# Weight splits without GpSimd, a gate applied to the product, and feed-forward rows scaled beforehand

## The chip, the cores and the metric

One core of one Trainium2 chip runs the kernel. The engines are named as the profile names them: PE is TensorE (PEld its weight loads), DVE VectorE, ACT ScalarE, POOL GpSimd, SP SyncE, which issues most DMAs. The metric is the device time of one execution in microseconds (us); the stated time is the median of three.

## The reference

Three transformer-like blocks follow one another on 256 rows of 1024 numbers, all in fp32. Cut to what matters here:

```python
def first_block(x, ...):                       # one layer
    proj = rms_norm(x, norm_w) @ w_in          # attention of two kinds, gates
    merged = sigmoid(gm) * (y_a @ w_branch_a) + sigmoid(gn) * (y_b @ w_branch_b)
    return x + merged @ w_out

def second_block(x, c, ctx, ...):              # two layers, m = six modulation vectors a layer
    h = h + m[2] * mixer(modulate(rms_norm(h), m[0], m[1]))   # layer 0: attention and convolution; layer 1: short convolution
    h = h + m[5] * ec_moe(modulate(rms_norm(h), m[3], m[4]))  # 16 experts, 32 rows each

def third_block(x, mem, ...):                  # two layers
    x = x + concat(mix, cross) @ w_out         # difference attention; gated linear attention
    x = x + conv_ffn(rms_norm(x, ffn_norm))

def conv_ffn(h, w_up, conv_w, conv_b, w_down):
    u = h @ w_up                               # 1024 -> 5632
    a, g = split(causal_conv_of_3_rows(u, conv_w) + conv_b)
    return (silu(g) * a) @ w_down              # 2816 -> 1024
```

The gate of the second block's mixers is m[2], a vector of 1024 by which the columns of a product are multiplied.

## The kernel before

**Dense products.** A dense weight is cut into groups of columns, and a group into slabs of up to 2048 floats a partition, each loaded by one DMA of SP into a ring of 4 (in the second block 7) places. `weights` (L384) cuts a slab into pieces of 1024 floats a partition and splits each: ACT casts it to the high half wh (fp32r, L378), and the low half wl = w - wh (L379) is made by DVE or by POOL. A counter decides (L404): of three splits POOL makes two, and in the difference attention, the third block's first mixer, all (`SHARES = 3, 2` and `DIFF_SHARES = 1, 1`). wh and wl have three buffers each. PE then does three products for each tile of 128 rows of the weight: high with high (L413), high with low (L414), low with high (L415). In `columns`, used by the feed-forward, the short convolution and others, the weight is the stationary operand and the 256 rows of data run through; in `rows` the data are stationary.

**The gate.** `residual` adds a product to x. Where a gate mrow is given (the mixers of the second block, ev_out and sc_out), `weights` multiplies each loaded slab in place by the gate's columns before it splits it: POOL the even slabs, DVE the odd ones (L395). The splits of such slabs are DVE's alone.

**The feed-forward** (`conv_ffn`, one for each layer of the third block). The rows x, times the norm's gain, are there turned and split (xh, xl), but not divided by their root mean square: this factor, rr, takes a chain of small operations on DVE (L532, L343 to L353), a product (ndiag) and a copy, and is applied to the product. The first products, called up, are done in 22 groups of 256 columns: 48 products for a group, into two PSUM banks (tag acc, of which there are three). For each bank DVE multiplies by rr into SBUF (ffu, L1941), ACT applies the third tap and the bias (ffc, L1943), and DVE adds the two other taps (L1944, L1945); then the two halves meet (ffh, L1949 to L1951) and are split into ff_h and ff_l (L381, L382). The second products, down, follow.

**Order.** The program is written engine by engine from a simulated schedule when it is built, so an engine's order isn't that of the code; each engine runs its own list strictly in order, and waits on semaphores.

Of the kernel before, what the change touches and what calls it, by code (L numbers as in the profile page):

```python
# [31 lines left out]
# Dense weights: (input name, layer, row order or None, column groups, k tiles a slab)  # L32
# [70 lines left out]
class Cols:  # L103
    """Columns of a [128, n] array: name -> slice."""
# [18 lines left out]
def _t5(n):  # L123
    # n < 16 exact, then the places where the logarithmic bucket steps up
    return n if n < 16 else min(15 + sum(n >= b for b in T5_STEPS), 31)
# [12 lines left out]
def _col(v):  # L138
    """A vector as [128, n]: element i*128+p at [p, i]."""
    return np.asarray(v).reshape(-1, 128).T  # L140


def _tables(i):
    """For each block, constants that depend on shapes alone and the small vectors and
    matrices, laid out for the partitions they are used on."""
# [90 lines left out]
# of so many splits of weights, how many GpSimd does  # L236
SHARES = 3, 2
# layer 0's slabs of modulation weights up to which the first block takes; those on VectorE; how many at a time
# [3 lines left out]
DIFF_SHARES = 1, 1  # L242


class Parts:
    """[128, 8, n] in tiles of its own for each few columns, so that they can take turns
    with those of another one of the same tag."""
# [13 lines left out]
class Later:  # L261
    """Parts from column k0 on."""
# [8 lines left out]
class Kern:  # L271
    def __init__(self, tc, ctx, a, tabs):
# [8 lines left out]
        self.fill, self.due, self.pace, self.nsplit, self.nslab, self.loads = None, 0, PACE[0], 0, 0, []  # L281
        self.tab, self.shares, self.hb = {}, SHARES, 1
# [39 lines left out]
    def slab(self, n):  # L322
        """The next place of n floats a partition in the ring of weights."""
        at = self.turn % sum(c for _, c in self.rings)
        self.turn += 1
        for pool, c in self.rings:
            if at < c:
                return pool.tile([128, 2048], F32, tag="w", name="w")[:, :n]
            at -= c

    def step(self, n=1):
        """Gives way to work that runs beside the products."""
# [6 lines left out]
    def newton(self, x, n, pool=None):  # L339
        """1 / sqrt(x)"""  # L340
# [15 lines left out]
    def rsqrt(self, ss, n, dim, pool=None):  # L356
        """1 / sqrt(ss / dim + EPS)"""
# [4 lines left out]
    def across(self, col, pool, name):  # L362
        """[128, n] -> PSUM [128, 128 * n]: element i * 128 + p along the rows of every partition."""
# [11 lines left out]
    def split(self, hi, lo, src, scale=1.0, eng=None):  # L375
        """hi + lo = scale * src, with hi and lo as the single-pass products take them."""
        if isinstance(scale, float) and scale == 1.0:
            self.nc.scalar.copy(hi, src)  # L378
            (eng or self.nc.vector).tensor_tensor(lo, src, hi.bitcast(F32), op=OP.subtract)  # L379
# [5 lines left out]
    def weights(self, key, g, chunks=None, by=None, gain=None):  # L385
        """Slabs of a column group, times a row [128, width] or a column [128, k tiles]:
        (k0, nk, width, high part, low part)."""
        for at, k0, nk, width in (OFF[key][g] if chunks is None else [OFF[key][g][c] for c in chunks]):
# [5 lines left out]
            if by is not None:  # L394
                (self.nc.vector if self.nslab % 2 else self.nc.gpsimd).tensor_tensor(w, w, by[:, None, :].to_broadcast([128, nk, width]), op=OP.mult)  # L395
            step = min(nk, 1024 // width)
            for k in range(0, nk, step):
# [3 lines left out]
                self.nsplit += 1  # L401
# [3 lines left out]
                else:  # L405
                    self.split(wh, wl, w[:, k:k + m], eng=self.nc.gpsimd if by is None and self.nsplit % self.shares[0] < self.shares[1] else None)
# [10 lines left out]
    def rows(self, key, g, xs, nkt, evac, ps=None, chunks=None, by=None, gain=None):  # L417
        """Rows of tokens: two tiles of 128 rows."""
# [4 lines left out]
        for k0, nk, width, wh, wl in self.weights(key, g, chunks, by, gain):  # L423
# [9 lines left out]
    def columns(self, key, g, xs, nkt, evac, m=128, n=S):  # L433
        """Columns of tokens: tiles of m outputs by 256 tokens (and what else the columns hold)."""
        width = OFF[key][g][0][3]
        ps = [self.acc(f"{key}{i}") for i in range(width // m)]
# [10 lines left out]
    def residual(self, key, xs, nkt, mrow=None, pool=None, hook=None, gain=None):  # L447
        """x += xs @ w (times mrow), and what the next norm needs of x."""
# [3 lines left out]
        def evac(g):  # L452
            def f(i, p):
                c = slice(512 * g, 512 * g + 512)
                nc.vector.tensor_tensor(self.x[:, i, c], self.x[:, i, c], p, op=OP.add)  # L455
# [7 lines left out]
        if nch == 2:  # L463
            ps = self.four(key)
            ps = [ps[:2], ps[2:]]
            for c in range(2):
                for g in range(2):
                    by = None if mrow is None else mrow[:, 512 * g:512 * g + 512]
                    self.rows(key, g, xs, nkt, evac(g) if c else None, ps[g], [c], by)
# [12 lines left out]
    def norm_state(self, pool=None, tag="xl", gain=None, fp=None, n=2, shift=None):  # L482
        """Sums of squares by tile and part (n of them), and the raw rows turned (in turns with the low part);
        with a gain [128, 8], their products with it instead, split at once, and a shift behind them, twice."""
# [8 lines left out]
    def norm_part(self, ns, x, g, w):  # L493
        """Columns w * g and on of x: [128, 2, D], or two tiles"""
# [43 lines left out]
    def norm_columns(self, ns, gain, shift, xh, pool):  # L538
        """The normed rows times gain, plus shift (each [128, 8]), turned and split."""
# [19 lines left out]
    def head_rstd(self, x, heads, dim, pool):  # L559
        """x [128, 2, heads * dim] -> [128, 2, heads]"""  # L560
# [13 lines left out]
    def turn_rows(self, out, rows, ncol, scale=None):  # L574
        """rows [128, 2, 128 * ncol] -> out [128, ncol, 256], times a column of scale."""
# [1417 lines left out]
```

## Time and profile before

| | us |
|---|---|
| median of three runs | 2323.93 |
| lowest and highest | 2321.32, 2329.56 |
| profiled execution, first to last instruction (span) | 2321.3 |
| its PE, DVE, ACT, POOL busy | 1861.8, 1086.4, 718.2, 574.5 |

The profile gives the span of one execution, and no time around it is shown apart; its 2321.3 stands beside the lowest run of 2321.32 and 2.6 below the median. Busy times are unions of an engine's instructions. A row that names a wait gives the engine that waited, its line, and what it waited for. PE's matmuls overlap their neighbours, so their steps from start to start say more than their durations.

### The profile page before, as it was taken

Reading aid. Unit: us, or ns where it says so; the run is one execution under the profiler, and the core shown is the slowest. Engines: PE = TensorE matmul, PEld = TensorE weight load, DVE = VectorE, ACT = ScalarE, POOL = GpSimd, SP = SyncE. Lnnn points to the kernel's source line nnn. Section 1 sums busy time; section 2 is a strip of 40 time slices with the busy share of each in tenths; the row PEclk is TensorE's granted clock in tenths of the full one; section 3 lists DMA queues with packets and bytes.
Section 4 is the critical chain, followed back from the end, with each engine's and each line's share of the span. In section 5 each row is a group of like instructions: output and inputs, shape, how many; then the busy total and the mean of one; then the engine's idle time right before and its main releaser. Section 6 shows DMA issues by size and latency. Waiting matters only on the chain. (4 is left out here: it accounts for less than half of the span.)

```text
span 2321.3 us, 35860 instructions
## 1 busy us (share of the span) xinstructions
PE 1861.8 (80%) x14677; PEld 1272.5 (55%) x14677; DVE 1086.4 (47%) x2124; ACT 718.2 (31%) x1352; POOL 574.5 (25%) x304
## 2 busy tenths in 40 slices
PE   6899988998666666797876665667889889898889
PEld 4777865564222222287532221225668887878887
DVE  5785666552100000187300000006857993777992
ACT  3345443341000000053200000005555554455553
POOL 3323353201000000044100000004334555434554
PEclk9999999999777777799986788778999999999999
DMA  8656578868999999994899999996424444334443
GB/s 224 237 200 214 186 281 303 317 235 336 408 408 408 409 405 408 393 388 148 338 407 408 408 408 405 409 400 238 137 91 145 154 155 169 110 123 153 157 151 121
DMA packets 176468, 638.01 MB, mean 275 GB/s; under 512 B 12158, under 2 KB 27390, under 8 KB 157872
## 3 DMA queue, kind: packets, MB, share of 16 engines
q1 hardware_dynamic: 173504, 627.03, 71.8%
q0 software_dynamic: 1360, 4.49, 1.2%
q10 hardware_dynamic: 1440, 4.21, 0.5%
q8 instruction: 115, 1.88, 0.3%
q14 instruction: 49, 0.40, 0.1%
HBM read 632.96 MB, written 2.72 MB: 274 GB/s over the span
## 5 line engine op out<-in xcount | busy, mean ns | idle before, releaser
L379 POOL TENSOR_TENSOR wl<-w,wh 128x1024 fp32r<-128x1024 f32 (+3 forms) x206 | 505.2, 2457 | 1544.2 <-ACT wh L378 1053.6
L378 ACT CAST wh<-w 128x1024 fp32r<-128x1024 f32 (+5 forms) x316 | 319.7, 1017 | 229.0 <-PE down L414 53.9
L1461 DVE SCALAR_TENSOR_TENSOR hd<-hd,gu 128x256 f32<-128x256 f32 x32 | 13.5, 421 | 491.2 <-ACT hd L1460 491.2
L1460 ACT ACTIVATE hd<-gu 128x256 f32<-128x256 f32 x32 | 12.3, 383 | 745.7 <-PE gu L1361 745.7
L413 PE MATMUL up<-xh,wh 128*128 128x256 f32 x704 | 196.7, 287 | 27.3 <-DVE ffu L1941 25.4
L379 DVE TENSOR_TENSOR wl<-w,wh 128x1024 fp32r<-128x1024 f32 (+3 forms) x110 | 152.4, 1386 | 121.7 <-ACT wh L378 121.6
L414 PE MATMUL up<-xh,wl 128*128 128x256 f32 x704 | 197.8, 285 | 11.7 <-DVE wl L379 11.7
L415 PE MATMUL up<-xl,wh 128*128 128x256 f32 x704 | 196.3, 284 | 1.0 <-DVE xl L379 1.0
L1361 PE MATMUL gu<-w,xst 128*32 128x256 f32 x1376 | 122.8, 490 | 67.8 <-DMA w<-in_moe_w_up 41.8
L1361 PE MATMUL gu<-more,xst 128*32 128x256 f32 x1344 | 108.1, 452 | 59.2 <-DMA more<-in_moe_w_up 34.3
L413 PEld LDWEIGHTS up<-xh,wh 128*128 128x128 f32 x704 | 132.1, 191 | 32.8 <-DVE ffu L1941 21.0
L414 PEld LDWEIGHTS up<-xh,wl 128*128 128x128 f32 x704 | 134.3, 191 | 14.9 <-DVE wl L379 14.6
L415 PEld LDWEIGHTS up<-xl,wh 128*128 128x128 f32 x704 | 133.7, 191 | 1.5 <-DVE xl L379 1.5
L1475 DVE SCALAR_TENSOR_TENSOR ysm<-dn,gcol,moe_mq 128x256 f32<-128x256 f32 x30 | 14.5, 484 | 235.5 <-PE dn L1361 235.5
L1361 PEld LDWEIGHTS gu<-w,xst 128*32 128x32 f32 x1376 | 44.9, 133 | 144.3 <-DMA w<-in_moe_w_up 69.5
L1361 PEld LDWEIGHTS gu<-more,xst 128*32 128x32 f32 x1344 | 42.8, 123 | 119.7 <-DMA more<-in_moe_w_up 55.8
L1945 DVE SCALAR_TENSOR_TENSOR ffc<-ffu,t,ffc 128x254 f32<-128x254 f32 x88 | 97.2, 1107 | 0.4
L1361 PE MATMUL dn<-more,ht 128*32 128x256 f32 x672 | 61.1, 514 | 16.0 <-DMA more<-in_moe_w_down 11.4
L413 PE MATMUL down<-wh,ff_h 128*128 128x512 f32 x176 | 69.7, 396 | 0.0
L414 PE MATMUL down<-wh,ff_l 128*128 128x512 f32 x176 | 69.5, 395 | 0.0
L1361 PE MATMUL dn<-w,ht 128*32 128x256 f32 x672 | 57.7, 485 | 12.7 <-DMA w<-in_moe_w_down 7.5
L415 PE MATMUL down<-wl,ff_h 128*128 128x512 f32 x176 | 63.6, 398 | 3.0 <-POOL wl L379 1.9
(634 smaller groups left out, 4198.6 us busy)
## 6 DMA issues: line engine op xcount, KB each, us to landing
w<-in_wd SPq DMA_DIRECT2D x144, 1024.0 KB, 5.0
w<-in_ada_w SPq DMA_DIRECT2D x48, 1024.0 KB, 6.6
w<-in_moe_w_gate SPq DMA_DIRECT2D x48, 1024.0 KB, 14.0
more<-in_moe_w_up SPq DMA_DIRECT2D x48, 1024.0 KB, 18.4
w<-in_moe_w_down SPq DMA_DIRECT2D x46, 1024.0 KB, 16.5
more<-in_moe_w_down SPq DMA_DIRECT2D x46, 1024.0 KB, 18.6
w<-in_moe_w_up SPq DMA_DIRECT2D x38, 1024.0 KB, 15.5
more<-in_moe_w_gate SPq DMA_DIRECT2D x36, 1024.0 KB, 18.5
```

Source lines behind the costliest of these rows:

```text
L378: self.nc.scalar.copy(hi, src)
L379: (eng or self.nc.vector).tensor_tensor(lo, src, hi.bitcast(F32), op=OP.subtract)
L413: mm(out, lh, rh, start=first, stop=False)
L414: mm(out, ll, rh, start=False, stop=False)
L415: mm(out, lh, rl, start=False, stop=last)
L1361: nc.tensor.matmul(out[32 * c:32 * c + 32], lhs(kt), w(1024 * kk + 256 * c, 256), start=kt == 0, stop=kt == 7, tile_position=(0, 32 * c))
L1460: nc.scalar.activation(hd, gu[:, 0:256], AF.Tanh, scale=0.5)
L1461: nc.vector.scalar_tensor_tensor(hd, hd, 1.0, gu[:, 0:256], op0=OP.add, op1=OP.mult)
L1475: nc.vector.scalar_tensor_tensor(y, dn[:, :256], gcol[:, e:e + 1], mq, op0=OP.mult, op1=OP.mult)
L1945: nc.vector.scalar_tensor_tensor(y[:, 2:], p[:, :S - 2], cw[:, ch, 0:1], y[:, 2:], op0=OP.mult, op1=OP.add)
```

## The change

GpSimd splits no weights: `split` loses its argument for the engine, and with it go SHARES, DIFF_SHARES and the counter. The gate goes from the slabs to `residual`: the product is multiplied out of PSUM into a tile mp, and that is added to x. In the feed-forward, four calls of `scaled` make the rows times rr, split again (sh, sl), behind the first three groups; from the fourth group on (RAW = 3) the products take these, and the convolution reads the product in PSUM, with no ffu. Odd groups take their two banks from another pool of PSUM (`gen`: four banks in all). Comments are taken out, so that line numbers shift by some lines.

```diff
-SHARES = 3, 2
-DIFF_SHARES = 1, 1
+RAW = 3
...
-    def split(self, hi, lo, src, scale=1.0, eng=None):
+    def split(self, hi, lo, src, scale=1.0):
         if isinstance(scale, float) and scale == 1.0:
             self.nc.scalar.copy(hi, src)
-            (eng or self.nc.vector).tensor_tensor(lo, src, hi.bitcast(F32), op=OP.subtract)
+            self.nc.vector.tensor_tensor(lo, src, hi.bitcast(F32), op=OP.subtract)
...
-            if by is not None:
-                (self.nc.vector if self.nslab % 2 else self.nc.gpsimd).tensor_tensor(w, w, by[:, None, :].to_broadcast([128, nk, width]), op=OP.mult)
...
-                self.nsplit += 1
...
-                    self.split(wh, wl, w[:, k:k + m], eng=self.nc.gpsimd if by is None and self.nsplit % self.shares[0] < self.shares[1] else None)
+                    self.split(wh, wl, w[:, k:k + m])
...
-    def columns(self, key, g, xs, nkt, evac, m=128, n=S):
+    def columns(self, key, g, xs, nkt, evac, m=128, n=S, ps=None):
...
-        ps = [self.acc(f"{key}{i}") for i in range(width // m)]
+        ps = [self.acc(f"{key}{i}") for i in range(width // m)] if ps is None else ps
...
     def residual(self, key, xs, nkt, mrow=None, pool=None, hook=None, gain=None):
...
                 c = slice(512 * g, 512 * g + 512)
+                if mrow is not None:
+                    m = pool.tile([128, 2, S], F32, tag="nf", name="mp", bufs=2).rearrange("p a s -> p (a s)")
+                    nc.vector.tensor_tensor(m, p, mrow[:, c], op=OP.mult)
+                    p = m
                 nc.vector.tensor_tensor(self.x[:, i, c], self.x[:, i, c], p, op=OP.add)
...
-                    by = None if mrow is None else mrow[:, 512 * g:512 * g + 512]
-                    self.rows(key, g, xs, nkt, evac(g) if c else None, ps[g], [c], by)
+                    self.rows(key, g, xs, nkt, evac(g) if c else None, ps[g], [c])
...
 def conv_ffn(k, l, ns, mem):
...
+        sh, sl = (pl.tile([128, 8, S], F32R, name=f"ff_x{z}") for z in "hl")
+
+        def scaled(j):
+            f, c = at.tile([128, 2, S], F32, tag="nf", name="ffs", bufs=2), slice(2 * j, 2 * j + 2)
+            nc.vector.tensor_tensor(f, xs[0][:, c].bitcast(F32), xs[1].part(j).bitcast(F32), op=OP.add)
+            nc.vector.tensor_tensor(f, f, rr[:, None, :].to_broadcast([128, 2, S]), op=OP.mult)
+            k.split(sh[:, c], sl[:, c], f)
...
-                u = at.tile([128, S], F32, tag="ffu", name="ffu")
-                nc.vector.tensor_tensor(u, p, rr, op=OP.mult)
-                p = u
+                if g < RAW:
+                    u = at.tile([128, S], F32, tag="ffu", name="ffu")
+                    nc.vector.tensor_tensor(u, p, rr, op=OP.mult)
+                    p = u
...
-            k.columns(f"up{l}", g, xs, 8, evac)
+            ps = [k.gen("up"), k.gen("up")] if g % 2 else None
+            k.columns(f"up{l}", g, xs if g < RAW else (sh, sl), 8, evac, ps=ps)
+            if g < RAW:
+                for j in range(4 * g // RAW, 4 * (g + 1) // RAW):
+                    scaled(j)
```

**DVE in the middle of the feed-forward of layer 0.** Its list before, over some ten operations:

```order
L1941 TENSOR_TENSOR ffu<-up_13504,ff_rr 128x256
L1950 SCALAR_TENSOR_TENSOR ffh<-ffh,ffc 128x256
L1951 TENSOR_TENSOR ffh<-ffh,ffc 128x256
L1944 SCALAR_TENSOR_TENSOR ffc<-ffu,t_11469,ffc 128x255
L1941 TENSOR_TENSOR ffu<-up_13505,ff_rr 128x256
L1945 SCALAR_TENSOR_TENSOR ffc<-ffu,t_11469,ffc 128x254
L382 SCALAR_TENSOR_TENSOR ff_l<-ffh,ff_h 128x256
L1944 SCALAR_TENSOR_TENSOR ffc<-ffu,t_11469,ffc 128x255
L1945 SCALAR_TENSOR_TENSOR ffc<-ffu,t_11469,ffc 128x254
L379 TENSOR_TENSOR wl<-w,wh 128x1024
```

The same place in the changed kernel (L377 is the split, L1951 and L1952 the two taps):

```order
L1951 SCALAR_TENSOR_TENSOR ffc<-up,t_11477,ffc 128x255
L377 TENSOR_TENSOR wl<-w,wh 128x1024
L380 SCALAR_TENSOR_TENSOR ff_l<-ffh,ff_h 128x256
L1951 SCALAR_TENSOR_TENSOR ffc<-up,t_11477,ffc 128x255
L1952 SCALAR_TENSOR_TENSOR ffc<-up,t_11477,ffc 128x254
L1957 SCALAR_TENSOR_TENSOR ffh<-ffh,ffc 128x256
L1952 SCALAR_TENSOR_TENSOR ffc<-up,t_11477,ffc 128x254
L1958 TENSOR_TENSOR ffh<-ffh,ffc 128x256
L377 TENSOR_TENSOR wl<-w,wh 128x1024
```

The two ffu of a group are gone, the taps read the product (up), and two splits stand among them.

**POOL at the end of the short convolution.** Before, with the two multiplications of slabs by the gate (sc_mrow):

```order
L1278 MEMSET scg 128x1
L379 TENSOR_TENSOR wl<-w,wh 128x1024 x3
L395 TENSOR_TENSOR w<-w,sc_mrow 128x2048
L379 TENSOR_TENSOR wl<-w,wh 128x1024
L395 TENSOR_TENSOR w<-w,sc_mrow 128x2048
L379 TENSOR_TENSOR wl<-w,wh 128x1024
L1429 TENSOR_TENSOR xr<-xf,xr 128x512 x2
```

In the changed kernel:

```order
L1275 MEMSET scg 128x1
L1276 MEMSET scg 128x1
L1275 MEMSET scg 128x1
L1276 MEMSET scg 128x1
L1427 TENSOR_TENSOR xr<-xf,xr 128x512 x2
```

Between the small memsets of the convolution's edges and the expert layer's first work (xr) nothing is left on POOL.

**DVE at the start of the feed-forward of layer 0**, from the norm's factor on. Before (ndiag is the factor on its way to rr):

```order
L369 TENSOR_TENSOR ndiag<-t_70,rs_y_12936 128x256
L379 TENSOR_TENSOR wl<-w,wh 128x1024
L1941 TENSOR_TENSOR ffu<-up_12958,ff_rr 128x256
L1941 TENSOR_TENSOR ffu<-up_12959,ff_rr 128x256
L1944 SCALAR_TENSOR_TENSOR ffc<-ffu,t_11469,ffc 128x255 x2
L1945 SCALAR_TENSOR_TENSOR ffc<-ffu,t_11469,ffc 128x254 x2
```

In the changed kernel:

```order
L367 TENSOR_TENSOR ndiag<-t_70,rs_y_12944 128x256
L377 TENSOR_TENSOR wl<-w,wh 128x1024 x2
L1948 TENSOR_TENSOR ffu<-up_12968,ff_rr 128x256
L1948 TENSOR_TENSOR ffu<-up_12969,ff_rr 128x256
L1934 TENSOR_TENSOR ffs<-ffs,ff_rr 128x512 x2
L1951 SCALAR_TENSOR_TENSOR ffc<-ffu,t_11477,ffc 128x255 x2
L377 TENSOR_TENSOR ff_xl<-ffs,ff_xh 128x512
L1952 SCALAR_TENSOR_TENSOR ffc<-ffu,t_11477,ffc 128x254
L377 TENSOR_TENSOR ff_xl<-ffs,ff_xh 128x512
L1952 SCALAR_TENSOR_TENSOR ffc<-ffu,t_11477,ffc 128x254
```

The scaled rows (ffs, ff_xl) of the first two parts stand among the first group's evacuation; those of the other two parts follow within the next 16 operations, and behind them the list is that of the first pair of listings.

## Rows read from the trace of the kernel before

**Rows 1.** The page: busy time of the engines, and POOL's splits.

```profile
PE 1861.8 (80%) x14677; PEld 1272.5 (55%) x14677; DVE 1086.4 (47%) x2124; ACT 718.2 (31%) x1352; POOL 574.5 (25%) x304
...
L379 POOL TENSOR_TENSOR wl<-w,wh 128x1024 fp32r<-128x1024 f32 (+3 forms) x206 | 505.2, 2457 | 1544.2 <-ACT wh L378 1053.6
```

**Rows 2.** Busy time by stretch: us, engines (count), PE clock, DMA share, GB/s.

```profile
517.00:993.00 476.00, 326.84 (x3480) 138.28 (x3478) 56.03 (x144) 32.58 (x81) 6.61 (x10) 0.78 1.01 397
993.00:1108.00 115.00, 100.70 (x711) 93.67 (x710) 91.25 (x109) 49.91 (x98) 53.56 (x34) 0.96 0.69 266
...
1587.00:1755.00 168.00, 145.95 (x674) 110.19 (x672) 121.22 (x322) 92.47 (x198) 69.98 (x34) 0.94 0.41 132
1755.00:1907.00 152.00, 132.53 (x1059) 128.17 (x1060) 143.26 (x218) 83.23 (x133) 75.20 (x29) 0.99 0.43 148
...
2101.00:2252.00 151.00, 132.30 (x1059) 128.05 (x1060) 141.48 (x216) 82.58 (x131) 73.95 (x28) 0.99 0.42 148
```

**Rows 3.** PE's waits, 1755 to 1907: total us, times, longest.

```profile
PE up L413 <- DVE ffu L1941: 12.7, 13, 1.4
PE up L414 <- DVE wl L379: 5.8, 7, 0.9
```

**Rows 4.** PE in order of time: start, duration, instruction, idle before.

```profile
1805.73 0.28 PE L413 MATMUL up<-xh,wh 128*128 128x256 f32 x1
...
1806.67 0.28 PE L415 MATMUL up<-xl,wh 128*128 128x256 f32 x1
...
1807.79 0.35 PE L413 MATMUL up<-xh,wh 128*128 128x256 f32 x1 [0.60 <-DVE ffu L1941]
...
1828.40 0.36 PE L413 MATMUL up<-xh,wh 128*128 128x256 f32 x1 [0.62 <-DVE ffu L1941]
```

**Rows 5.** POOL and DVE in order of time, at two places.

```profile
1851.06 3.03 POOL L379 TENSOR_TENSOR wl<-w,wh 128x1024 fp32r<-128x1024 f32 x1 [2.81 <-ACT wh L378]
...
1851.78 2.60 DVE L1945 SCALAR_TENSOR_TENSOR ffc<-ffu,t,ffc 128x254 f32<-128x254 f32 x1
...
1859.86 0.48 DVE L1945 SCALAR_TENSOR_TENSOR ffc<-ffu,t,ffc 128x254 f32<-128x254 f32 x1
1860.26 1.22 DVE L379 TENSOR_TENSOR wl<-w,wh 128x1024 fp32r<-128x1024 f32 x1
1861.39 0.42 DVE L1941 TENSOR_TENSOR ffu<-up,ff_rr 128x256 f32<-128x256 f32 x1
1861.73 0.42 DVE L1950 SCALAR_TENSOR_TENSOR ffh<-ffh,ffc 128x256 f32<-128x256 f32 x1
```

**Rows 6.** Tile ffu, 1755 to 1907: ns, least, median, most.

```profile
L1941 DVE TENSOR_TENSOR ffu<-up,ff_rr x42: 408/414/423, 1767.4 to 1903.2; 128x256 f32<-128x256 f32 x42
...
L1945 DVE SCALAR_TENSOR_TENSOR ffc<-ffu,t,ffc x41: 468/473/2645, 1769.4 to 1906.6; 128x254 f32<-128x254 f32 x41
```

**Rows 7.** The short convolution: tile sc_mrow on POOL, and PE's waits 993 to 1108.

```profile
L395 POOL TENSOR_TENSOR w<-w,sc_mrow x2: 4766/5694/6623, 1055.8 to 1065.3; 128x2048 f32<-128x2048 f32 x2
...
PE sc_out L413 <- ACT sc_yh L378: 4.8, 1, 4.8
PE sc_in L414 <- DVE wl L379: 3.3, 1, 3.3
PE sc_in L413 <- ACT sc_s L1269: 2.5, 1, 2.5
```

**Rows 8.** PE's waits in 0 to 332, 332 to 517 and 1587 to 1755.

```profile
PE tr L582 <- DVE qn L570: 2.9, 1, 2.9
PE out L415 <- POOL wl L379: 2.7, 1, 2.7
...
PE tr L582 <- DVE ev_w L1208: 6.9, 1, 6.9
...
PE tr L582 <- DVE dn L570: 3.7, 2, 2.9
```

More of the change, by code (lines that the diff above doesn't have):

```diff
@@ L280, in __init__ @@
         self.gens, self.gturn = [(self.ps, PS_BUFS["gen"])], 0
-        self.fill, self.due, self.pace, self.nsplit, self.nslab, self.loads = None, 0, PACE[0], 0, 0, []
-        self.tab, self.shares, self.hb = {}, SHARES, 1
+        self.fill, self.due, self.pace, self.nslab, self.loads = None, 0, PACE[0], 0, []
+        self.tab, self.hb = {}, 1
         self.load_table("t0")
@@ L382, in split, with weights @@
             self.nc.vector.scalar_tensor_tensor(lo, src, scale, hi.bitcast(F32), op0=OP.mult, op1=OP.subtract)
-    def weights(self, key, g, chunks=None, by=None, gain=None):
+    def weights(self, key, g, chunks=None, gain=None):
         for at, k0, nk, width in (OFF[key][g] if chunks is None else [OFF[key][g][c] for c in chunks]):
@@ L415, in mm3, with rows @@
         mm(out, lh, rl, start=False, stop=last)
-    def rows(self, key, g, xs, nkt, evac, ps=None, chunks=None, by=None, gain=None):
+    def rows(self, key, g, xs, nkt, evac, ps=None, chunks=None, gain=None):
         width = OFF[key][g][0][3]
@@ L422, in rows @@
         xh, xl = xs
-        for k0, nk, width, wh, wl in self.weights(key, g, chunks, by, gain):
+        for k0, nk, width, wh, wl in self.weights(key, g, chunks, gain):
             for i, p in enumerate(ps):
@@ L1669, in dr @@
             return at.tile([128, 2, 512], F32, tag="dr", name="dqr", bufs=2)
-        k.hb, k.shares = 2, DIFF_SHARES
+        k.hb = 2
         raw = [dr()]
@@ L1760, in diff_mixer @@
         finish(2, 4, 4)
-        k.shares, k.hb = SHARES, 1
+        k.hb = 1
 def gla_mixer(k, xs, rs, mem, yh, yl):
```

## The prediction

> **What bounds the kernel now.** I read the page first for the engines' shares: TensorE (PE) is busy 1861.8 of 2321.3 us, VectorE (DVE) 1086.4, GpSimd (POOL) 574.5 [rows 1]. An average over stages says little, so I then cut the span where the dense products change. Two stretches of some 480 us (one stands in [rows 2], 517 to 993) are the expert layers: the DMA share is 1.01 at 397 GB/s, and POOL does 6.6 us there. The change touches nothing in them, so they stay as they are. In the other stretches shown DMA runs at 132 to 266 GB/s, and PE is the busiest or nearly so. The two that stand out are the feed-forward's first products, 1755 to 1907 and 2101 to 2252: DVE is busy 143.3 of 152 and 141.5 of 151 us, PE only 132.5 and 132.3.
>
> The waits of PE in the first of these say why [rows 3]: 12.7 us for ffu, the multiplication by which DVE empties a PSUM bank (13 times), and 5.8 us for wl, the low half of a split of weights that DVE made (7 times). PE's own order in time shows how regular this is [rows 4]: undisturbed, eight steps from 1805.73 to 1806.67 take 0.94 us, 0.118 each; but from one wait for ffu at 1807.79 to its like at 1828.40, three column groups (144 products) take 20.6 us where 144 x 0.118 = 17.0 would do.
>
> DVE is full because of POOL, not of its own work. At 1851.06 POOL starts a split of 3.03 us; the ffc that DVE starts at 1851.78 lasts 2.60 us, until POOL is done, while the same operation at 1859.86, with POOL idle, lasts 0.48 [rows 5]. Over the stage that line has a median of 473 ns and a maximum of 2645, and the multiplication ffu, which has one input in PSUM, never exceeds 423 [rows 6]. So what is held up is an operation with both inputs in SBUF while POOL runs a split.
>
> **The change, part by part.**
>
> *Splits.* A split on POOL takes some 2.5 us and holds DVE up for as much. On DVE it starts at 1860.26 and the next operation at 1861.39 [rows 5]: 1.13 us of the queue. Per column group of the feed-forward there are two splits, so DVE gets 2 x 1.13 = 2.26 us, of which a third is there already.
>
> *No ffu from the fourth group on.* The two multiplications go; the convolution reads PSUM instead. No row has this operation from PSUM. Bounds: ffu, which does read PSUM, takes 408 to 423 ns, ffc from SBUF 473 [rows 6], so it is 0.41 to 0.47; I take the upper, 0.40 us of the queue (1859.86 to 1860.26 in [rows 5]). DVE's group is then 2.26 + 4 x 0.40 (ffc) + 3 x 0.34 (ffh twice and ff_l, by the step of a 256-column operation from 1861.39 to 1861.73) = 4.9 us. PE's is 48 x 0.118 = 5.7. PE becomes the bound, DVE at 85% of it. PSUM banks are held longer, but odd groups take theirs from another pool, so seven banks serve where three did.
>
> *The scaled rows.* Each layer adds 12 operations of 128x512 on DVE (addition, multiplication, low half, for four parts), some 0.6 us each, a little over half of a 1024-column split's step: 7.3 us, and four casts on ACT. They stand in DVE's queue with seven splits of weights and the first groups' evacuations (the third order listing); from the norm's sum to the last ff_xl I add 7.3 + 7 x 1.13 + 8 x 0.40 + some 6 of small ones = 25 us. PE needs the second half of group 3 after three and a half groups, 20 us. New wait: 5 us in each layer, between 0 (if PE is late itself) and 8.
>
> *One stage.* 1056 products x 0.12 (the pace rounded up) = 127, plus 5, plus 1 for the xl at the start: 133. Now 152 and 151: **-19 and -18**. The bounds: 127, and 143, where half of the present waits return in another form.
>
> *The gate.* Before, four slabs of each gated product are multiplied in place, 128x2048 on POOL and DVE in turn. In the short convolution the two on POOL take 4.8 and 6.6 us [rows 7], at 1055 to 1072, just when PE waits 3.3 us for wl, 2.5 for sc_s and 4.8 for sc_yh. Those waits are 10.6 us; with the eleven microseconds of POOL and DVE's own two multiplications gone, I count **-10**: nearly all of them and some smaller ones there, less a chain of some 2 us (an estimate of five short steps) from the last column to the first output product, which stays. The new multiplication leaves PSUM with 512 columns, 0.6 us by half a split; tiles end at different times, so only the last tile's is on the path: **+0.6** for each of the two blocks, with 0 and 2.4 as bounds.
>
> *The first block* (0 to 332): PE waits 2.7 us for a split of POOL, the longest of four such waits, and 2.9 for qn, a DVE operation of two SBUF inputs [rows 8]. A split on DVE is 1.4 us shorter, but it stands behind other work: **-8** of this and its like, bounds 0 and -15. *The even mixer*: 6.9 us for a chain that crosses DVE and POOL [rows 8]; POOL no longer has splits ahead of it: **-3**. *The difference attention*: 3.7 us for dn: **-3**; all of its splits come to DVE, which is busy 121 of 168 us there now [rows 2], with about as much freed as added.
>
> **Sum**: -19 -18 -10 +1.2 -8 -3 -3 = -60. The profiled span of 2321.3 becomes 2261.5; the runs' median, 2323.93, lies 2.6 above that span, so I predict **2264**.
>
> **The rivals.**
>
> *A queue in order.* On POOL a split may wait for its cast at no one's cost; on DVE everything behind it waits too. The cast waits for PE to free a buffer (three stand in turn), and takes about 1 us. If each split loses x at the head of DVE's queue, a group costs 4.9 + 2x: from x = 0.4 DVE bounds the stage, at x = 1 the gain is gone. Before, DVE's 14 splits lost little in this stage, since it was behind anyhow (its queue is busy 94%), so the trace doesn't exclude it; against it, the splits are spread among the evacuations in the new order. With x about 0.7 a group is 6.3 us and a stage 143: 2 x 9 = 18, and half of the other 23, some 30 in all: **2294**.
>
> *All waits go.* The feed-forward at 127 twice (49), the short convolution's 14, the first block's 15, and others: some 90, **2234**.
>
> *DVE is the bound* (slower). If DVE's length is its own, the 28 splits come on top: 143.3 + 28 x 1.13 - 38 x 0.34 + 7 = 169 us a stage, +17 twice, and DVE-heavy attention stages +5 each: some **2370**. It decides where DVE's work in a group exceeds 6.9 us (20.6 / 3) instead of 4.9, so where an ffc unhindered by POOL still took twice 0.40 and more. Against it is the median of 473 against the maximum. The Trainium skill (Perfetto Trace Analysis, Optimizing Scalar/DVE Operations) states a rule that speaks for this rival: with DVE saturated, work may be moved away from it, even to GpSimd, with the caution that the two share a port. By its first half, taking work back to a DVE that is 94% busy is wrong and the time would be this rival's 2370; by its second half, and by the two ffc in [rows 5], the busy share is itself made by sharing. The trace bears out the second.
>
> *The product is held by PSUM*: ffu emptied a bank early, now it is held through three operations and ACT. With seven banks a group has two groups' time, 11 us, for a chain of about 4; this can cost only if the scheduler puts them late. I count it into the first rival.
>
> **How the numbers follow.** Likeliest: PE bounds the feed-forward, 2240 to 2285, chance 0.57, at 2264. All waits go, below 2240: 0.12. The queue in order eats half, 2285 to 2317: 0.18. Same, within 0.3% (7 us, which is about what these runs can tell apart): 0.05. Slower: 0.08. Faster is 0.57 + 0.12 + 0.18 = 0.87. The range of 8 in 10 is 2232 to 2312: it leaves out 0.13 above and some 0.06 below.
>
> **What would show it.** In the profile after: POOL has no wl; the maximum of ffc near its median; DVE's total about as before or less (some 1050) though it has 206 more splits [rows 1]; PE's waits in the feed-forward below 8 us a stage, one of them near the fourth group; the period of three groups 17 to 18 us. Wrong would be: PE waits for wl by ten or more times a stage, DVE idle before wl for ACT's cast (the first rival), or ffc above 0.6 us with POOL idle (the third). The expert stretches should keep their 476 us.

## The result, and the profile after

The changed kernel takes 2251.62 us (median of four runs, 2248.91 to 2254.34) beside 2326.74 of the kernel before on the same chip: ratio 0.9674, 95% interval 0.9653 to 0.9695, faster. The span of its profiled execution is 2252.5 us, 68.8 less than before; 59.8 less were forecast (2261.5). The medians lie 75.1 apart, since the profiled execution before is the shortest of its four and the one after the longest.

The page, busy time of the engines and the group of all splits, answers to [rows 1]:

```profile
PE 1853.4 (82%) x14677; PEld 1275.5 (57%) x14677; DVE 1026.7 (46%) x2282; ACT 723.6 (32%) x1360; POOL 53.0 (2%) x94
...
L377 DVE TENSOR_TENSOR wl<-w,wh 128x1024 fp32r<-128x1024 f32 (+5 forms) x316 | 377.3, 1198 | 172.5 <-ACT wh L376 165.7
```

DVE has 158 instructions more, POOL's splits among them, and is busy 60 us less. Busy time by stretch, as in [rows 2] (the first expert layer in two pieces, short convolution, difference attention, the two stages of first products):

```profile
515.90:559.00 43.10, 32.27 (x251) 21.75 (x255) 21.18 (x62) 14.46 (x33) 6.78 (x10) 0.84 0.67 239
559.00:999.40 440.40, 295.18 (x3236) 117.27 (x3226) 37.46 (x87) 19.10 (x50) 0.00 (x0) 0.78 1.03 406
999.40:1094.50 95.10, 94.61 (x698) 90.18 (x697) 72.56 (x123) 48.87 (x95) 0.93 (x16) 1.00 0.82 314
1578.00:1736.60 158.60, 143.50 (x674) 109.93 (x672) 122.01 (x346) 93.24 (x200) 9.20 (x8) 0.94 0.43 140
1736.60:1869.50 132.90, 129.38 (x1059) 128.33 (x1060) 121.03 (x228) 85.89 (x139) 0.00 (x0) 0.97 0.48 169
2055.10:2185.20 130.10, 127.16 (x1059) 126.68 (x1060) 119.31 (x223) 85.50 (x137) 0.00 (x0) 0.99 0.49 171
```

In 1736.6 to 1869.5 DVE does 22 us less than in [rows 2], with 29 splits more. The tile ffc there (compare [rows 6]) shows why: the taps are never held up.

```profile
L1951 DVE SCALAR_TENSOR_TENSOR ffc<-up,t,ffc x37: 470/477/483, 1770.0 to 1869.3; 128x255 f32<-128x255 f32 x37
L1952 DVE SCALAR_TENSOR_TENSOR ffc<-up,t,ffc x36: 468/474/485, 1772.1 to 1865.0; 128x254 f32<-128x254 f32 x36
```

PE's waits in the same stage, where [rows 3] had 12.7 for ffu and 5.8 for wl, and all of PE's waits in the short convolution, 999.4 to 1094.5, where [rows 7] had 4.8, 3.3 and 2.5 among others:

```profile
PE up L409 <- DVE wl L377: 1.8, 1, 1.8
PE up L410 <- DVE ff_xl L377: 1.2, 1, 1.2
PE up L408 <- ACT ff_xh L376: 0.3, 1, 0.3
...
PE sc_in L410 <- DVE xl L377: 0.2, 1, 0.2
PE sc_in L408 <- DVE scc L1271: 0.2, 1, 0.2
```

Where the 68.8 us came from, by the first and last dense products of each stage in PE's order in time (us, each from the profiled execution; Q, G, R and QG are experiments below: GpSimd quiet, that is without splits, alone; gate alone; rows alone; quiet and the gate in the short convolution alone). Each column is one execution, and some us in one stage can be chance: in G and R, whose edits lie behind it, the first block takes 339.6 and 337.8 where before has 332.0.

| stage | before | after | forecast | Q | G | R | QG |
|---|---|---|---|---|---|---|---|
| first block | 332.0 | 325.3 | -8 | 328.7 | 339.6 | 337.8 | 325.2 |
| even mixer | 184.7 | 190.6 | -3 | 189.0 | 196.1 | 184.9 | 191.3 |
| first expert layer | 476.2 | 483.5 | 0 | 477.6 | 481.8 | 478.0 | 476.6 |
| short convolution | 114.6 | 95.1 | -10 | 101.7 | 99.8 | 113.5 | 95.0 |
| second expert layer | 479.5 | 483.5 | 0 | 484.5 | 481.6 | 481.2 | 483.5 |
| difference attention | 168.0 | 158.6 | -3 | 154.9 | 173.4 | 172.3 | 159.6 |
| first products, layer 0 | 152.1 | 132.9 | -19 | 127.5 | 150.6 | 143.5 | 127.4 |
| gated linear attention | 129.4 | 123.3 | 0 | 122.6 | 132.1 | 128.6 | 124.3 |
| first products, layer 1 | 151.2 | 130.1 | -18 | 126.7 | 149.6 | 142.7 | 126.7 |

The two stages of second products (down) gave 2 us each.

### The profile page after: what moved, and what is told of

Same layout as the page of the kernel before. It is cut to its first block, busy times and chain, and to the rows that moved or that the text cites. A ratio compares the mean times of both kernels' runs of the same rounds, so it can differ in the third digit from the quotient of the medians.

```text
span 2252.5 us, 35590 instructions
## 1 busy us (share of the span) xinstructions
PE 1853.4 (82%) x14677; PEld 1275.5 (57%) x14677; DVE 1026.7 (46%) x2282; ACT 723.6 (32%) x1360; POOL 53.0 (2%) x94
## 4 chain that ended last, share of the span: by engine, by line
PE 51%; DMA 37%; DVE 6%; ACT 3%; issue 2%; SPq 0%; POOL 0%; ACTq 0%; DVEq 0%
DMA w<-in_moe_w_up 6%; DMA more<-in_moe_w_gate 4%; DMA wl<-in_moe_w_up 4%; PE up L410 4%; PE up L409 4%; PE up L408 4%; DMA more<-in_moe_w_up 3%; PE gu L1359 3%; DMA w<-in_moe_w_down 3%; DMA more<-in_moe_w_down 2%; PE down L408 2%; PE down L410 2%; PE down L409 2%; DMA wl<-in_moe_w_down 2%; DVE wl L377 2%
## 5 line engine op out<-in xcount | busy, mean ns | idle before, releaser
L377 DVE TENSOR_TENSOR wl<-w,wh 128x1024 fp32r<-128x1024 f32 (+5 forms) x316 | 377.3, 1198 | 172.5 <-ACT wh L376 165.7
L409 PE MATMUL up<-ff_xh,wl 128*128 128x256 f32 x608 | 171.0, 283 | 2.7 <-DVE wl L377 2.7
L410 PE MATMUL up<-ff_xl,wh 128*128 128x256 f32 x608 | 170.1, 283 | 1.2 <-DVE ff_xl L377 1.2
L408 PE MATMUL up<-ff_xh,wh 128*128 128x256 f32 x608 | 168.5, 284 | 2.4 <-ACT ff_xh L376 2.4
L409 PEld LDWEIGHTS up<-ff_xh,wl 128*128 128x128 f32 x608 | 116.2, 191 | 3.1 <-DVE wl L377 3.1
L410 PEld LDWEIGHTS up<-ff_xl,wh 128*128 128x128 f32 x608 | 115.2, 190 | 1.5 <-DVE ff_xl L377 1.5
L408 PEld LDWEIGHTS up<-ff_xh,wh 128*128 128x128 f32 x608 | 114.4, 191 | 2.8 <-ACT ff_xh L376 2.8
L1359 PE MATMUL dn<-more,ht 128*32 128x256 f32 x672 | 56.3, 483 | 14.1 <-DMA more<-in_moe_w_down 9.6
L409 PE MATMUL w_in_b<-xh,wl 128*128 128x256 f32 x192 | 56.4, 295 | 2.8 <-DVE wl L377 2.8
L408 PE MATMUL w_in_b<-xh,wh 128*128 128x256 f32 x192 | 55.2, 296 | 2.0 <-ACT wh L376 2.0
## 6 DMA issues: line engine op xcount, KB each, us to landing
w<-in_moe_w_up SPq DMA_DIRECT2D x38, 1024.0 KB, 15.6
```

Of the source, the lines that this page charges most:

```text
L377: self.nc.vector.tensor_tensor(lo, src, hi.bitcast(F32), op=OP.subtract)
L408: mm(out, lh, rh, start=first, stop=False)
L409: mm(out, ll, rh, start=False, stop=False)
L410: mm(out, lh, rl, start=False, stop=last)
L1359: nc.tensor.matmul(out[32 * c:32 * c + 32], lhs(kt), w(1024 * kk + 256 * c, 256), start=kt == 0, stop=kt == 7, tile_position=(0, 32 * c))
```

## The experiments

The theory: GpSimd's splits hold DVE up, and quieting them is the gain. The main rival: DVE's length is its own, and the scaled rows relieve it.

**1. GpSimd quiet (Q).** The kernel before, all splits on DVE, nothing else.

```diff
-self.split(wh, wl, w[:, k:k + m], eng=self.nc.gpsimd if by is None and self.nsplit % self.shares[0] < self.shares[1] else None)
+self.split(wh, wl, w[:, k:k + m], eng=None)
```

> The kernel before, with all splits of weights on DVE; GpSimd still multiplies slabs by the gate, and the feed-forward still has ffu in all groups. Theory (GpSimd's splits hold DVE up): DVE's group in the feed-forward is then 2 x 1.13 + 2 x 0.40 + 4 x 0.40 + 3 x 0.34 = 5.7 us, about PE's own 5.7, so a first-product stage takes 135 to 142 us instead of 152, and with the first block's gain the whole some 2285. Rival (DVE's length is its own, and the rows are what relieves it): 28 splits x 1.13 more on a full queue, a stage of some 169 us, the whole 2340 to 2370.

Measured: 2240.25 us, ratio 0.9606 (0.9574 to 0.9638): this one line is worth more than the whole change, and more than was expected of it (2285, and 135 to 142 us for a stage). The first products of layer 0, by stretch:

```profile
1736.40:1863.90 127.50, 126.27 (x1059) 125.58 (x1060) 122.90 (x248) 83.94 (x133) 0.00 (x0) 1.00 0.50 176
```

And one column group of DVE in order of time:

```profile
1801.10 1.23 DVE L379 TENSOR_TENSOR wl<-w,wh 128x1024 fp32r<-128x1024 f32 x1
1802.24 0.42 DVE L1941 TENSOR_TENSOR ffu<-up,ff_rr 128x256 f32<-128x256 f32 x1
1802.57 0.42 DVE L382 SCALAR_TENSOR_TENSOR ff_l<-ffh,ff_h 128x256 fp32r<-128x256 f32 x1
...
1806.77 1.22 DVE L379 TENSOR_TENSOR wl<-w,wh 128x1024 fp32r<-128x1024 f32 x1
```

DVE's group takes 5.67 us (1801.10 to 1806.77), ffu and all, which is the sum of the expectation (5.7), and PE's own is 48 x 0.118 = 5.66 by [rows 4]. DVE is busy 96% of the stage, and PE waits 1.5 us in it (1.0 of it for ffu). The rival, with a stage of 169 us, falls.

**2. The gate alone (G).** The kernel before, with the multiplication in `residual`.

```diff
+                if mrow is not None:
+                    m = pool.tile([128, 2, S], F32, tag="nf", name="mp", bufs=2).rearrange("p a s -> p (a s)")
+                    nc.vector.tensor_tensor(m, p, mrow[:, c], op=OP.mult)
+                    p = m
...
-                    by = None if mrow is None else mrow[:, 512 * g:512 * g + 512]
+                    by = None
```

> The kernel before, with only the gate moved from the slabs to the product. Theory: the short convolution loses the waits behind GpSimd's two multiplications, 10 to 15 of its 114.6 us; the first expert layer starts with a later norm and takes some 7 us more as in the changed kernel; the whole about 2318. Rival (the gate's place costs nothing at the expert layer, that loss has another cause): expert layer 476, the whole about 2310.

Measured: 2331.96 us, ratio 1.0012 (0.9996 to 1.0028): no change, where 2318 was expected. The short convolution fell by 14.8, within the expected 10 to 15, and the first expert layer rose by 5.6. So the rest was lost elsewhere. The profiled execution, the slowest of ten and 8 us above the kernel's median, is longer by 7.6 in the first block, ahead of the edit, by 11.4 in the even mixer and by 5.4 in the difference attention; how much of that the edit makes is not shown. Its short convolution:

```profile
1017.50:1117.30 99.80, 96.03 (x702) 90.66 (x701) 76.57 (x102) 48.81 (x95) 52.05 (x37) 1.00 0.79 302
```

GpSimd still splits there (52.05 us, x37). Not only PE's idle time fell, but its busy time too, from 100.70 us at a granted clock of 0.96 [rows 2] to 96.03 at 1.00.

**3. The rows alone (R).** The kernel before, with `scaled` and the two more banks; GpSimd still splits.

```diff
+RAW = 3
...
-                u = at.tile([128, S], F32, tag="ffu", name="ffu")
-                nc.vector.tensor_tensor(u, p, rr, op=OP.mult)
-                p = u
+                if g < RAW:
+                    u = at.tile([128, S], F32, tag="ffu", name="ffu")
+                    nc.vector.tensor_tensor(u, p, rr, op=OP.mult)
+                    p = u
...
-            k.columns(f"up{l}", g, xs, 8, evac)
+            ps = [k.gen("up"), k.gen("up")] if g % 2 else None
+            k.columns(f"up{l}", g, xs if g < RAW else (sh, sl), 8, evac, ps=ps)
```

> The kernel before, with only the scaled rows of the feed-forward and the two more PSUM banks; GpSimd still splits two of three pieces of weights. Theory (holding by GpSimd is what fills DVE): 38 ffu x 0.4 go and some 7 us come, DVE stays held up, a stage of 143 to 150 us, the whole 2308 to 2322. Rival (fewer operations on DVE are the gain, whoever splits): the stage falls to some 133 as in the changed kernel, the whole about 2287.

Measured: 2309.35 us, ratio 0.9904 (0.9872 to 0.9936), stages of 143.5 and 142.7, as the theory had it. Tile ffc (and ffh), 1767 to 1911:

```profile
L1954 DVE SCALAR_TENSOR_TENSOR ffc<-up,t,ffc x36: 469/474/484, 1803.6 to 1908.5; 128x255 f32<-128x255 f32 x36
L1955 DVE SCALAR_TENSOR_TENSOR ffc<-up,t,ffc x36: 468/482/485, 1805.5 to 1909.0; 128x254 f32<-128x254 f32 x36
...
L1961 DVE TENSOR_TENSOR ffh<-ffh,ffc x20: 408/426/2623, 1795.2 to 1905.7; 128x256 f32<-128x256 f32 x20
```

With GpSimd splitting beside them, the taps are no longer held up, since one of their inputs is now in PSUM; ffh, with both in SBUF, still is. So the rows shelter a part of DVE's work from GpSimd: by the count explained in the next section it is held up for 37 us in this stage, where before it was 52. They also leave DVE less to do, 38 ffu gone for 12 operations of the rows; how the 8.6 us divide between the two is not shown. What they are worth where GpSimd is quiet, experiment 4 tells.

**4. The change without the rows.** RAW = 22, no `scaled`, the two more banks kept.

```diff
-RAW = 3
+RAW = 22
...
-            k.columns(f"up{l}", g, xs if g < RAW else (sh, sl), 8, evac, ps=ps)
-            if g < RAW:
-                for j in range(4 * g // RAW, 4 * (g + 1) // RAW):
-                    scaled(j)
+            k.columns(f"up{l}", g, xs, 8, evac, ps=ps)
```

> The changed kernel without the scaled rows: ffu in all 22 groups, the two more PSUM banks kept. Theory: DVE's group is 5.7 us, as long as PE's; the stage takes 135 to 142 us instead of 131.5 on average, the whole 2260 to 2272. Rival (the rows carry the feed-forward's gain): the stages return to 152 and 151, the whole 2292.

Measured: 2244.69 us, ratio 0.9628 (0.9597 to 0.9658); the stages take 128.9 and 128.4, less than with the rows. Both expectations missed (135 to 142 us, and 152): leaving the rows out loses nothing, it gains (the interval just overlaps that of the changed kernel; the stages say it more clearly).

**5 and 6. GpSimd disturbs, and nobody uses what it makes.** Experiment 1, and in the first products an instruction on GpSimd for two of three splits, into an unread tile: in 5 the subtraction once more, in 6 a copy, with one input.

```diff
+                    if key[:2] == "up" and self.nsplit % 3 < 2:
+                        z = self.spare[:, :m * width].rearrange("p (k c) -> p k c", c=width)
+                        self.nc.gpsimd.tensor_tensor(z, w[:, k:k + m], wh.bitcast(F32), op=OP.subtract)
...
+                        self.nc.gpsimd.tensor_copy(z, wh)
```

> The first experiment's kernel (all splits on DVE), and in the feed-forward's first products GpSimd does two of three subtractions a second time, into a tile that nobody reads; so no work leaves DVE and nothing on the path waits for GpSimd but the reuse of buffers. Theory (a split on GpSimd holds up DVE's operations with both inputs in SBUF for some 2.5 us): 29 splits a stage hold DVE up by 1.5 to 2.5 us each, 45 to 70 us, so a stage goes from 127.5 to 165 or more, the whole to some 2320 or above. Rival (GpSimd's splits were late, but held nothing up): the stage stays at 127.5, the whole at 2240.

> As the run before, but GpSimd only copies the high half into the unread tile: one input in SBUF instead of two. If any reading of SBUF by GpSimd holds DVE's two-input operations up, the stage is again far above 127.5 (145 to 170, by the copy's own length); if only GpSimd's operations with two inputs do, the stage stays at 127 to 130 and the whole at 2240.

Measured: 2362.18 us for 5 (ratio 1.0146, 1.0126 to 1.0165), stages of 188.8 and 185.3 instead of 127.5 and 126.7; 2268.25 for 6 (0.9742, 0.9723 to 0.9761), stages of 139.9 and 139.8. POOL and DVE of experiment 5 in order of time:

```profile
1802.88 5.94 POOL L409 TENSOR_TENSOR ff_z<-w,wh 128x1024 fp32r<-128x1024 f32 x2 [7.64 <-ACT wh L378]
...
1803.92 0.42 DVE L1945 TENSOR_TENSOR ffu<-up,ff_rr 128x256 f32<-128x256 f32 x1
1804.26 2.29 DVE L382 SCALAR_TENSOR_TENSOR ff_l<-ffh,ff_h 128x256 fp32r<-128x256 f32 x1
1806.48 0.41 DVE L1945 TENSOR_TENSOR ffu<-up,ff_rr 128x256 f32<-128x256 f32 x1
1806.81 3.09 DVE L379 TENSOR_TENSOR wl<-w,wh 128x1024 fp32r<-128x1024 f32 x1
```

And what PE waits for most, 1738 to 1912:

```profile
PE up L417 <- DVE wl L379: 32.0, 16, 3.6
```

ff_l takes 2.29 instead of 0.42 and the split 3.09 instead of 1.22, while ffu between them, under the same instructions of POOL, keeps its 0.41. The trace shows no wait of PE, ACT or DVE in this stage for POOL or for a DMA, so what POOL reads was not late in being free again. By the count of the next section DVE is held up for 56 us in a stage that is 61 longer; PE is longer idle, and also longer busy, 145.43 us at a granted clock of 0.91 instead of 126.27 at 1.00. In experiment 6 the tile ff_z and the tap:

```profile
L409 POOL CAST ff_z<-wh x27: 1042/1300/2132, 1739.2 to 1862.2; 128x1024 fp32r<-128x1024 f32 x27
...
L1949 DVE SCALAR_TENSOR_TENSOR ffc<-ffu,t,ffc x42: 469/473/1296, 1745.5 to 1871.7; 128x254 f32<-128x254 f32 x42
```

One input suffices, and the hold lasts up to the length of GpSimd's instruction: 1.30 us for the copy, some 2.6 for the split. The bounds for 6 were somewhat high (139.9 where 145 was the least).

The Trainium skill (SBUF — State Buffer, Who interferes with whom) says that a VectorE instruction with two SBUF inputs contends with a GpSimd instruction that reads SBUF, that one with at most one SBUF input doesn't outside the 2-port modes, and that the lock lasts a whole instruction. These traces agree on each point: 2.29 against 0.42, ffu at 0.41, a tap of 1.296 under copies of 1.30.

**7. The gate on the product in the short convolution alone (QG).** Experiment 1, and the gate as in the change where the key is sc_out, on the slabs where it is ev_out.

```diff
+                if mrow is not None and key == "sc_out":
...
+                    by = None if mrow is None or key == "sc_out" else mrow[:, 512 * g:512 * g + 512]
```

> The first experiment's kernel with the gate on the product in the short convolution alone, and on the slabs in the even mixer. Theory (the gate on the product takes the waits in the short convolution away, but delays the norm ahead of the first expert layer): short convolution 95 us as in the changed kernel instead of 101.7, first expert layer 477, the whole some 2234. Rival (the difference of the expert layer is chance): short convolution 95, expert layer 482, the whole 2240.

Measured: 2238.83 us, ratio 0.9614 (0.9600 to 0.9628). Both stages came out as the theory had them (95.0 and 476.6), the whole didn't: the difference attention took 159.6 instead of 154.9, which gave most of it back. So it can't be told from experiment 1; both beat the changed kernel by some 12 us. With GpSimd quiet that stage takes 154.3 to 154.9 in the three kernels that have the gate of sc_out on the slabs (experiments 1, 5, 6), and 156.2 to 160.5 in the six that have it on the product; why is open.

**8. Scaled rows later.** The changed kernel with RAW = 5.

> The changed kernel with the scaled rows from the sixth group on instead of the fourth (RAW = 5), so that their parts are spread over five groups. Theory (the stage's rest over 127.5 is the wait for the scaled rows and the lower clock behind it): the wait goes or falls below 1 us, the granted clock stays at 1.00, the stages take 128 to 130 instead of 132.9 and 130.1, the whole some 2247. Rival (the 24 more operations on a full DVE cost this wherever they stand): the stages stay as they are, the whole 2251.

Measured: 2243.79 us, ratio 0.9645 (0.9621 to 0.9668). Layer 1 takes 127.5 and has no wait for scaled rows, as the theory has it. Layer 0 takes 132.8, as the rival has it, and waits for a split of weights instead (wl 2.2, wh 1.2), with a granted clock of 0.93 and 0.90 in the 20 us around. The operations are a cost that can be spread but doesn't always hide.

**9 and 10. The gate's product in PSUM.** The multiplication writes its bank back instead of mp: in 9 in the changed kernel, in 10 in experiment 1 with the gate of both blocks on the product.

```diff
-                    m = pool.tile([128, 2, S], F32, tag="nf", name="mp", bufs=2).rearrange("p a s -> p (a s)")
-                    nc.vector.tensor_tensor(m, p, mrow[:, c], op=OP.mult)
-                    p = m
+                    nc.vector.tensor_tensor(p, p, mrow[:, c], op=OP.mult)
```

> The changed kernel with the gate's product written back to its PSUM bank instead of into the SBUF tile mp; the number of operations is the same. Theory (mp lies where the first expert layer's tile own is later put, so that a load of weights waits for the last reader of mp, and all loads behind it in SP's queue with it): own is issued right behind the load ahead of it, the first expert layer takes 478 to 480 us instead of 483.5, the whole some 2247. Rival (the layer is late because the norm comes 2.4 us later): the layer stays at 482 to 484, the whole 2251.

> The first experiment's kernel (all splits on DVE, ffu in all groups, no scaled rows, no more PSUM banks) with the gate of both blocks applied to the product in its PSUM bank. Theory: short convolution 95 us, first expert layer 478 to 480, first products of the feed-forward 127; the whole 2233 to 2240, below both kernels. Rival (the later norm keeps the first expert layer at 482 or more): 2240 to 2245, no better than the first experiment.

Measured: 2249.50 us for 9 (ratio 0.9658, 0.9619 to 0.9697) and 2243.72 for 10 (0.9633, 0.9600 to 0.9665). In 9 the load into own goes out at 516.70, right behind the one ahead of it, instead of at 520.08 in the changed kernel, yet the first expert layer takes 482.2, and 482.7 in 10. The theory on mp falls, and the times are the rival's. That the norm's own delay is what costs does not follow from this; the next section reads from the traces what does.

## Why the prediction was right, and where it wasn't

**What bounds the kernel: right, and more so than it said.** Taking away the hold by GpSimd is most of the gain. Taking every DVE operation that overlaps one of POOL, and its duration less the median of its like that overlap none, gives some 270 us in the trace of before and some 8 in that of after (264 to 284 and 5 to 10, by how narrowly "its like" is taken). By stage, before: first block some 56, even mixer 16, short convolution 31, difference attention 28, first products 52 and 52, gated linear attention 16. Experiments 1 and 5 show the cause from both sides. The third rival (DVE's length is its own) falls with them.

**First products, -19 and -18: right sum (-19.2, -21.1), wrong parts.** The step that failed is the one that needs the missing ffu to bring DVE from 5.7 to 4.9 us a group. A DVE queue as long as PE's is short enough: experiment 1 has 5.67 beside 5.66, and stages of 127.5 and 126.7, the time of PE alone. The tap from PSUM cost the 0.40 that was taken (0.39 from start to start, median duration 474 ns), but the missing ffu saved nothing that PE felt. What the rows do is the **new wait near the fourth group**, forecast at 5 us a layer. DVE in order of time:

```profile
1758.44 1.21 DVE L377 TENSOR_TENSOR wl<-w,wh 128x1024 fp32r<-128x1024 f32 x1
1759.57 0.41 DVE L1948 TENSOR_TENSOR ffu<-up,ff_rr 128x256 f32<-128x256 f32 x1
1759.91 0.41 DVE L1957 SCALAR_TENSOR_TENSOR ffh<-ffh,ffc 128x256 f32<-128x256 f32 x1
1760.24 0.68 DVE L1934 TENSOR_TENSOR ffs<-ffs,ff_rr 128x512 f32<-128x512 f32 x1
```

And busy time by stretch, with the granted clock behind POOL's column:

```profile
1755.00:1760.00 5.00, 3.21 (x27) 3.01 (x26) 5.00 (x9) 2.92 (x4) 0.00 (x0) 1.00 0.23 70
1760.00:1765.00 5.00, 3.49 (x19) 2.99 (x19) 5.00 (x10) 2.25 (x4) 0.00 (x0) 0.62 0.70 261
1765.00:1770.00 5.00, 5.00 (x33) 5.00 (x32) 3.71 (x10) 2.11 (x5) 0.00 (x0) 0.70 0.22 90
1770.00:1775.00 5.00, 5.00 (x44) 5.00 (x43) 4.94 (x9) 4.40 (x8) 0.00 (x0) 1.00 0.02 5
```

DVE has no gap, and PE's 1.8 us are for the split at 1758.44, which stands behind scaled rows; 1.2 and 0.3 for these themselves follow. Between these waits the granted clock falls toward the lower level: 33 products in the 5 us from 1765 where 44 is the pace, and 19 in the 3.49 us of work before that where 31 would be, so some 1.3 us lost in each. The fall is not certain: in experiment 9, with the same feed-forward, PE waits 1.8, 0.3 and 1.8 us at this place, the clock stays at 1.00, and the stage takes 131.3. Against experiment 4 the rows cost 132.9 - 128.9 = 4.0 us in layer 0 (2.4 in experiment 9) and 130.1 - 128.4 = 1.7 in layer 1: mis-sized for the second.

**Short convolution, -10: mis-sized, -19.5.** The term summed PE's named waits, 10.6 us, with some smaller ones, and kept a chain of some 2. PE's idle time fell by more, from 14.3 us (115.00 - 100.70, [rows 2]) to 0.5 (95.10 - 94.61), and nothing of the chain was left. Its busy time, which the term left out, fell by 6 from 100.70 to 94.61, with the granted clock at 1.00 instead of 0.96. The hold of DVE alone doesn't tell the price: the gate alone keeps it (29 us by the same count) and still gives -14.8. Quiet alone gives -12.9, both -19.5: the two overlap, and end where PE is busy for nearly the whole stage.

**The gate, +0.6 each: mis-sized at the first expert layer.** The term counted the last tile's multiplication only. All six kernels of this study with the slabs' gate at ev_out have that layer at 475.5 to 478.0, all six with the product's at 481.8 to 483.5. PE, ACT, DVE and SP's queue of the changed kernel in order of time:

```profile
525.94 2.74 PE L1316 MATMUL router<-wg,xl 128*128 128x16 f32 x12 [1.09 <-ACT xl L515]
...
531.76 5.59 PE L1388 MATMUL y<-x,t 128*128 128x512 f32 x8
...
523.19 1.70 ACT L1425 ACTIVATE xf<-x,rs_y 128x256 f32<-128x256 f32 x4 [2.21 <-DVE rs_y L351]
524.80 0.60 ACT L1426 CAST xr<-xf 128x512 fp32r<-128x512 f32 x1
525.31 0.57 ACT L515 COPY xl<-nt 128x512 f32<-128x512 f32 x1
...
516.94 1.28 DVE L452 TENSOR_TENSOR mp<-ev_out,ev_mrow 128x512 f32<-128x512 f32 x2
...
537.42 0.38 SPq L1350 DMA_DIRECT2D x<-in_moe_w_down  x1
```

The same of before, with the row of its first 43 us:

```profile
518.53 4.10 PE L1318 MATMUL router<-wg,xl 128*128 128x16 f32 x32
...
525.84 4.96 PE L1390 MATMUL y<-x,t 128*128 128x512 f32 x8
...
519.35 0.57 ACT L517 COPY xl<-nt 128x512 f32<-128x512 f32 x1
521.65 1.70 ACT L1427 ACTIVATE xf<-x,rs_y 128x256 f32<-128x256 f32 x4 [1.73 <-DVE rs_y L353]
...
530.87 0.38 SPq L1352 DMA_DIRECT2D x<-in_moe_w_down  x1
...
516.70:560.00 43.30, 36.56 (x342) 22.70 (x344) 19.24 (x58) 13.66 (x33) 6.61 (x10) 0.88 0.82 309
```

Four multiplications of 0.6 us stand among the additions, so the last turned columns come late, and their copy xl, which the router needs, now stands on ACT behind the scaling of rows (xf, xr); before, it stood ahead of it. The router's product ends at 528.68 instead of 522.63, y starts 5.9 us later, and the load of weights that takes the place of the tile x, and waits for y, goes out 21.5 us after the end of ev_out instead of 14.2 (537.42 - 515.9, 530.87 - 516.7). In SP's queue the other loads stand behind it, in a layer that DMA bounds: 440.4 us at 406 GB/s, after 43 us at 239 where the kernel before had 309. What was not moved in these 43 us takes (309 - 239) x 43 / 406 = 7.4 us later, which is what the layer rose by. The same two groups of six kernels show it at each step: y starts 9.1 to 9.3 us after the end of ev_out with the slabs' gate and 14.7 to 15.9 with the product's, that load goes out after 14.0 to 15.6 and 19.7 to 22.4, and the first 43 us run at 305 to 308 GB/s and 239 to 256. In experiments 9 and 10 the router ends earlier, 7.9 us after ev_out instead of 12.8, but another step of this chain is then behind xr on ACT (PE waits 6.4 us). That this chain sets the layer's end is read from the traces; no run moved one link alone.

**First block -8:** -6.7, within its bounds. **Even mixer -3: wrong, +5.9.** The wait for ev_w is 7.2 us where it was 6.9 [rows 8], so POOL's splits had no part in it, and PE waits 2.9 for frec (0.6 before) and 1.6 for another ev_w (none before). With quiet GpSimd and the old gate there (experiments 1, 5, 6, 7) it is +4.3 to +6.6, so the gate is not its cause; why it is longer is open. **Difference attention -3** was -9.4 and **gated linear attention**, with no term, -6.1: PE's waits on POOL's splits were short there, but quiet alone gives -13.1 and -6.8: DVE's hold was some 28 and 16 us, and the terms for it were 3 and nothing. **Expert layers "keep their 476 us": wrong**; the second rose by 4.0. Where the gate of sc_out is on the product its first 43 us run at 280 to 291 GB/s instead of 313 before, which is worth 2.3 to 3.5 us by the same sum. In experiments 1, 5 and 6 they run at 310 to 313 and the layer still takes 483.1 to 484.5; that cause is open.

So -60 came out as -69. The terms that were too small (short convolution, two attentions) were so by 22 us together, those that were too kind (even mixer, expert layers, with the gate's own +1.2 taken off) by 19, and the first products and the rest make up the remaining 6. That the whole came so near is in part luck, since 22 and 19 nearly cancel; what bounds the kernel was not.

None of the rivals occurred in the changed kernel. DVE waits 9.4 us for wh in the first products of layer 0, 18 times, which is 0.2 a split and not the 0.7 of the queue in order. The second rival, in which all waits go, is what experiment 1 comes near, with 127.4 and 126.7 in the first products.

## What to carry to other kernels

Before work is moved from VectorE to GpSimd, look at VectorE's longest durations beside its medians: an operation on two SBUF inputs that sometimes takes as long as GpSimd's instruction is paid for twice. Test the parts of such a change one by one: here one line gave more than the whole, and an edit that helped before (the rows) cost time once the cause was gone. A multiplication of 0.6 us in front of a norm is priced by what stands in order behind that norm, not by its own length.

## What the hardware showed that I had not expected

A GpSimd copy with a single input holds VectorE as a subtraction does, for its own 1.30 us. VectorE at 96% busy kept TensorE at its own pace for 127 us (PE waited 1.5). And in the changed kernel three waits of 1.8, 0.3 and 1.2 us, close together in a stage at full clock, went with a granted clock of 0.62 and 0.70 over 10 us, between its two levels (1.2 and 2.4 GHz), before it was back at 1.00; in experiment 9 waits of 1.8, 0.3 and 1.8 at the same place left it at 1.00.
